# Gathered rows of a PEER feed-forward: a nearer place in the scheduler's order during the dense pass, and 5.15 instead of 5.25 rows per chunk

## The chip, the cores and the metric

One core of a Trainium2 chip runs the whole program. The metric is the device time of one execution in microseconds (us). The engines are TensorE (PE, whose weight loads are shown apart as PEld), VectorE (DVE), ScalarE (ACT), GpSimd (POOL) and SyncE (SP). SP issues the plain transfers and POOL the indirect ones; both kinds share the core's 16 DMA engines.

## What is computed

One decoder block on 1024 tokens of width 1024, in float32: two token mixers (stick-breaking attention and a gated delta rule) are merged by sigmoid gates, and a PEER feed-forward follows. For each token PEER picks 8 x 16 = 128 of 16384 experts, and adds their outputs, weighted by a gate and an exact GELU:

```
def block(args):
    hb, eb, gb = args                 # 128 tokens
    u = u_tab[eb]                     # 128 rows of 1024 for each token
    act = jax.nn.gelu(jnp.einsum('td,ted->te', hb, u), approximate=False)
    v = v_tab[eb]
    return jnp.einsum('te,ted->td', gb * act, v)
```

## The kernel before

The 1024 tokens are eight blocks of 128. PEER is done in two ways at once.

**Dense, blocks 2, 3, 6 and 7 (`dense`, L854).** All 16384 experts are evaluated for 512 tokens, and a table of gates that is zero for the experts not picked weighs them. There are 128 steps of 128 experts. A step has 24 matmuls of scores (L885, L887), a GELU on ACT (L889), a multiplication by the gates on DVE (`weigh`, L915) and a split of the product into two float32r halves, the high one on ACT (L919), the low one on DVE (L906), and 24 matmuls with V (`mm3`, L72 to L74). U and V arrive in 512 KB transfers, and each is split the same way (`split`, L63 on ACT, L64 on DVE). The loop over `k` (L966) has two `k` per step, and this pair is a **chunk**. After every eight `k`, four chunks, four accumulators of TensorE are added into `d_acc` by four DVE instructions (L974): the work between two such quads is a **group** below. TensorE can't write on before they are done, since six banks serve four accumulators.

**Gathered, blocks 0, 1, 4 and 5 (`gather_rows`, L993).** For each of the 128 picks of a block, POOL issues an indirect DMA that brings one row of U for each token (L1016, 128 rows of 4 KB, 512 KB), and DVE multiplies it with the hidden state and sums along it (L1019); this is a **u row**. After 128 of them a GELU follows (L1007) and a multiplication by the gates (L1009), and then 128 **v rows**, each an indirect DMA and a DVE instruction that adds into an accumulator (L1021). Below, a **row** is one such pair. There are 4 x 256 = 1024. The hidden state (from `h2d`) and the accumulator (from `x2d`) share one buffer, `gb_h`; when a block goes from u to v rows, or one block follows another, DVE waits for the load of the other. Rows land in buffers that are used in turn: four, `gb_row0` to `gb_row3`, and two more, `gb_row4` and `gb_row5`, while the dense loop runs (L961, L988). POOL issues in order, and a row's transfer starts once DVE has finished the row that had its buffer before.

**What sets the order.** The rows have no place of their own: `gather(phase)` (L1045) is called from every phase, adds `PACE[phase]` (L31) to a debt and emits one row for each whole unit of it. In the dense loop it is called once per chunk (L985), before that in the table of gates (L850), among others. A scheduler then orders each engine: of the instructions that are ready in its own reckoning it takes the one with the lowest number, and an instruction's number is the place at which it was emitted. `later(n)` (L46) adds n to the numbers of what is emitted inside it. Rows got 1000000, so that anything else that was ready went first. `behind` (L1032) keeps a row's DVE instruction behind the last DVE instruction that was emitted before it. The call without a phase, after the dense pass, emits the rows that are left, with no addition and, by then, four buffers.

Of the kernel before, what the change touches and what calls it, by code (L numbers as in the profile page):

```python
# [27 lines left out]
CB = 256  # L28
EPS = 1e-6

PACE = dict(sb=2.2, gdn=1.5, logits=2.5, merge=2.5, out=0.5, route=0, table=0.1, dense=5.25)  # L31
NEG = -1e30
C_Q, C_K, C_V = 0, 1024, 2048
C_GQ, C_GK, C_GV, C_GZ = 3072, 4096, 5120, 6144
# [4 lines left out]
class Block:  # L39
# [1005 lines left out]
    def gather(self, phase=None):  # L1045

        if self.rows is None:
            return
        if phase is None:
            self.anchor = None  # L1050
            for _ in self.rows:
                pass
            return
        self.due += PACE[phase]
        self.anchor = self.last_dve()
        with self.later(1000000):
            while self.due >= 1:
                self.due -= 1
                next(self.rows, None)
# [119 lines left out]
```

## Time and profile before

| | |
|---|---|
| median of 3 runs | 3876.8 us (3871.88 to 3877.51) |
| the profiled execution | 3877.26 us |
| its span, first to last instruction | 3875.4 us |
| dense pass, last quad of the gate tables to the end | about 2380 to 3875 us |
| first and last accumulation into `d_acc` (L974) | 2458 and 3853 us |

The profiled execution stands 0.5 us above the median. All moments below are us from the start of the span. A row of the timeline gives start, duration, engine, line, operation, output and inputs, the number of merged instructions, and in brackets the idle time of the engine before it with what ended it.

### The profile page before, as it was taken

What the parts mean: (1) busy time and instruction counts of PE and PEld (TensorE: products, weight loads), DVE (VectorE), ACT (ScalarE), POOL (GpSimd) and SP (SyncE); (2) the same over time, 40 slices, a digit from 0 to 9 for tenths busy, and PEclk for the clock granted to TensorE, in tenths of its full rate; (3) what the DMA queues carried; (4) which work ended last, traced back from release to release, by engine and by line L of the source; (5) the groups of instructions that cost most, each with busy time, mean ns of one, the idle gap of its engine ahead of it and who ended that gap; (6) DMA issues with size and microseconds to landing.
All of it is one profiled execution on the core that took longest, in us unless ns stands there. A gap on an engine that the chain in (4) does not pass through costs nothing.

```text
span 3875.4 us, 53560 instructions
## 1 busy us (share of the span) xinstructions
PE 3596.4 (93%) x18936; PEld 2983.8 (77%) x18936; DVE 3077.5 (79%) x6196; ACT 1740.7 (45%) x3846; POOL 1356.6 (35%) x1034
## 2 busy tenths in 40 slices
PE   8999999999999999998878877999999999999996
PEld 7878888788777688886667666787778787788785
DVE  5345554349988878888879998899898899899898
ACT  6755554333777655553322786222222322222221
POOL 0000000000044332223442003666666665676665
PEclk9999999999999999999989999999999999999998
DMA  4221113553377756558985568999999999999998
GB/s 121 88 82 50 55 50 115 174 186 93 96 256 265 246 191 192 191 182 290 325 307 170 158 185 289 353 361 358 334 365 358 345 371 365 348 364 374 353 359 312
DMA packets 344205, 937.49 MB, mean 242 GB/s; under 512 B 41984, under 2 KB 121088, under 8 KB 339712
## 3 DMA queue, kind: packets, MB, share of 16 engines
q0 software_dynamic: 147456, 536.94, 38.8%
q1 hardware_dynamic: 196480, 397.13, 30.1%
q8 instruction: 149, 2.44, 0.3%
q14 instruction: 120, 0.98, 0.1%
HBM read 864.22 MB, written 69.21 MB: 241 GB/s over the span
## 4 chain that ended last, share of the span: by engine, by line
PE 42%; issue 20%; POOL 12%; DVE 11%; DMA 10%; ACT 4%; SPq 0%; POOLq 0%; DVEq 0%; ACTq 0%
POOL gb_row L1016 12%; PE mm L72 6%; PE mm L74 6%; PE mm L73 6%; DMA gb_row<-peer_v,expert 5%; PE pc L848 3%; DMA gb_row<-peer_u,expert 3%; PE mm L885 2%; PE pz L532 2%; PE pz L526 2%; DVE gb_row L1019 2%; DVE w_lo L64 2%; PE mm L887 1%; PE pc L317 1%; PE pz L295 1%
## 5 line engine op out<-in xcount | busy, mean ns | idle before, releaser
L1016 POOL DMA_INDIRECT gb_row<-peer_u,expert x512 | 693.6, 1355 | 1848.2 <-DVE expert L793 1012.8
L1016 POOL DMA_INDIRECT gb_row<-peer_v,expert x512 | 661.9, 1293 | 656.4 <-DVE gb_h L1021 408.8
L1019 DVE SCALAR_TENSOR_TENSOR gb_row<-gb_row,gb_h 128x1024 f32<-128x1024 f32 x512 | 614.0, 1219 | 133.2 <-DMA gb_row<-peer_u,expert 109.7
L1021 DVE SCALAR_TENSOR_TENSOR gb_h<-gb_row,gb_act,gb_h 128x1024 f32<-128x1024 f32 x512 | 657.7, 1285 | 73.7 <-DMA gb_row<-peer_v,expert 50.4
L885 PE MATMUL mm<-hf,ut 128*128 128x512 f32 x2048 | 491.2, 391 | 6.9 <-DMA hf<-hd 6.9
L919 ACT CAST d_a<-u_act 128x512 fp32r<-128x512 f32 x128 | 79.2, 621 | 926.5 <-DVE u_act L915 917.7
L885 PEld LDWEIGHTS mm<-hf,ut 128*128 128x128 f32 x2048 | 386.1, 189 | 87.7 <-issue 7.6
L64 DVE TENSOR_TENSOR w_lo<-w_raw,w_hi 128x512 fp32r<-128x512 f32 (+1 forms) x450 | 297.6, 682 | 163.9 <-ACT w_hi L63 125.9
L63 ACT CAST w_hi<-w_raw 128x512 fp32r<-128x512 f32 (+1 forms) x450 | 262.1, 620 | 286.2 <-PE mm L73 122.6
L72 PE MATMUL mm<-h,w_hi 128*128 128x512 f32 (+1 forms) x784 | 322.9, 412 | 3.0 <-ACT pj L598 3.0
L74 PE MATMUL mm<-h,w_lo 128*128 128x512 f32 (+1 forms) x784 | 320.6, 409 | 0.0
L73 PE MATMUL mm<-h,w_hi 128*128 128x512 f32 (+1 forms) x784 | 319.7, 408 | 0.0
L72 PE MATMUL pz<-d_v,d_a 128*128 128x512 f32 x680 | 272.8, 401 | 41.2 <-DVE d_acc L974 30.1
L72 PE MATMUL mm<-w_hi,h 128*128 128x256 f32 x1024 | 299.8, 293 | 8.5 <-DVE x L647 5.7
L74 PE MATMUL mm<-w_hi,h 128*128 128x256 f32 x1024 | 294.0, 288 | 4.0 <-DVE h L64 4.0
L73 PE MATMUL mm<-w_lo,h 128*128 128x256 f32 x1024 | 295.1, 288 | 1.0 <-DVE w_lo L64 0.9
L74 PE MATMUL pz<-d_v,d_a 128*128 128x512 f32 x680 | 270.4, 398 | 0.0
L73 PE MATMUL pz<-d_v,d_a 128*128 128x512 f32 x680 | 270.4, 398 | 0.0
L887 PE MATMUL mm<-hf,ut 128*128 128x512 f32 x1024 | 257.0, 391 | 2.5 <-DVE ut L64 2.5
L887 PEld LDWEIGHTS mm<-hf,ut 128*128 128x128 f32 x1024 | 192.8, 188 | 42.8 <-DVE ut L64 3.3
L72 PEld LDWEIGHTS mm<-w_hi,h 128*128 128x128 f32 x1024 | 199.5, 195 | 16.3 <-DVE x L647 6.4
L73 PEld LDWEIGHTS mm<-w_lo,h 128*128 128x128 f32 x1024 | 199.7, 195 | 6.7 <-issue 3.8
(327 smaller groups left out, 7947.9 us busy)
## 6 DMA issues: line engine op xcount, KB each, us to landing
w_raw<-w_in SPq DMA_DIRECT2D x144, 512.0 KB
u_raw<-u_t SPq DMA_DIRECT2D x128, 512.0 KB
v_raw<-v_t SPq DMA_DIRECT2D x128, 512.0 KB
g_d<-gt_stg SPq DMA_DIRECT2D x16, 2048.0 KB
d_g<-g_d SPq DMA_DIRECT2D x31, 1024.0 KB
w_raw<-peer_w_q SPq DMA_DIRECT2D x32, 512.0 KB
gl<-pj SPq DMA_DIRECT2D x32, 256.0 KB
th<-gl SPq DMA_DIRECT2D x32, 256.0 KB
```

What stands on the lines that cost most here:

```text
L63: nc.scalar.copy(hi, src)
L64: nc.vector.tensor_tensor(lo, src, hi.bitcast(F32), op=OP.subtract)
L72: mm(out, l[0], r[0], start=first, stop=False)
L73: mm(out, l[0], r[1], start=False, stop=False)
L74: mm(out, l[1], r[0], start=False, stop=last)
L848: self.last_gate = mm(pg[:, u - u0], o2[:, u], o1[:, u], start=True, stop=True)
L885: mm(ps, ut[0][:, k], hx[a][:, k, x0:], start=k + a == 0, stop=False)
L887: mm(ps, ut[1][:, k], hx[0][:, k, x0:], start=False, stop=k == KD - 1)
L919: nc.scalar.copy(hi, act)
L1016: nc.gpsimd.indirect_dma_start(out=r, out_offset=None, in_=self.i["peer_u" if p < n else "peer_v"][0], in_offset=bass.IndirectOffsetOnAxis ...
L1019: i = nc.vector.scalar_tensor_tensor(r, r, 1.0, h2, op0=OP.mult, op1=OP.mult, accum_out=act[:, q:q + 1])
L1021: i = nc.vector.scalar_tensor_tensor(acc, r, act[:, q:q + 1], acc, op0=OP.mult, op1=OP.add)
```

## The change

In the dense pass alone the rows' numbers are raised by 800 instead of 1000000, and the debt grows by 5.15 per chunk instead of 5.25. Everything else of the program is as it was; the counts on every engine are the same.

```
-PACE = dict(sb=2.2, gdn=1.5, logits=2.5, merge=2.5, out=0.5, route=0, table=0.1, dense=5.25)
+PACE = dict(sb=2.2, gdn=1.5, logits=2.5, merge=2.5, out=0.5, route=0, table=0.1, dense=5.15)
...
         self.due += PACE[phase]
         self.anchor = self.last_dve()
-        with self.later(1000000):
+        with self.later(800 if phase == "dense" else 1000000):
             while self.due >= 1:
                 self.due -= 1
                 next(self.rows, None)
```

PE's and POOL's orders keep their forms, DVE's moves in many places. Three of them are shown, with buffer numbers.

**Start of the dense loop, DVE.** `gb_row1_22120` and `gb_row2_22380` were emitted in the gate tables, so they keep 1000000; the rows from `gb_row3_22834` on come from the dense loop. Before:

```order
L1019 SCALAR_TENSOR_TENSOR gb_row2_22380,gb_act_17073<-gb_row2_22380,gb_h2_17071 128x1024
L1019 SCALAR_TENSOR_TENSOR gb_row3_22834,gb_act_17073<-gb_row3_22834,gb_h2_17071 128x1024
L1019 SCALAR_TENSOR_TENSOR gb_row4_22837,gb_act_17073<-gb_row4_22837,gb_h2_17071 128x1024
L1019 SCALAR_TENSOR_TENSOR gb_row1_22828,gb_act_17073<-gb_row1_22828,gb_h2_17071 128x1024
L1019 SCALAR_TENSOR_TENSOR gb_row5_22840,gb_act_17073<-gb_row5_22840,gb_h2_17071 128x1024
L64 TENSOR_TENSOR d_v1_22846<-v_raw_22843,d_v0_22845 128x1024
L64 TENSOR_TENSOR ut1_22876<-u_raw_22873,ut0_22875 128x1024
L64 TENSOR_TENSOR d_v1_22929<-v_raw_22926,d_v0_22928 128x1024
L1019 SCALAR_TENSOR_TENSOR gb_row2_22831,gb_act_17073<-gb_row2_22831,gb_h2_17071 128x1024
L1019 SCALAR_TENSOR_TENSOR gb_row0_22911,gb_act_17073<-gb_row0_22911,gb_h2_17071 128x1024
L1019 SCALAR_TENSOR_TENSOR gb_row1_22914,gb_act_17073<-gb_row1_22914,gb_h2_17071 128x1024
```

Now:

```order
L1019 SCALAR_TENSOR_TENSOR gb_row1_22120,gb_act_17073<-gb_row1_22120,gb_h2_17071 128x1024
L64 TENSOR_TENSOR d_v1_22846<-v_raw_22843,d_v0_22845 128x1024
L64 TENSOR_TENSOR ut1_22876<-u_raw_22873,ut0_22875 128x1024
L64 TENSOR_TENSOR d_v1_22929<-v_raw_22926,d_v0_22928 128x1024
L1019 SCALAR_TENSOR_TENSOR gb_row4_22923,gb_act_17073<-gb_row4_22923,gb_h2_17071 128x1024
L1019 SCALAR_TENSOR_TENSOR gb_row1_22828,gb_act_17073<-gb_row1_22828,gb_h2_17071 128x1024
L1019 SCALAR_TENSOR_TENSOR gb_row2_22380,gb_act_17073<-gb_row2_22380,gb_h2_17071 128x1024
L64 TENSOR_TENSOR ut1_22959<-u_raw_22956,ut0_22958 128x1024
L915 TENSOR_TENSOR u_act_22904<-u_act_22904,d_g_22759 128x512
L906 TENSOR_TENSOR d_a1_22908<-u_act_22904,d_a0_22907 128x512
L1019 SCALAR_TENSOR_TENSOR gb_row1_22914,gb_act_17073<-gb_row1_22914,gb_h2_17071 128x1024
```

The two early rows, and with them whatever follows in buffers 1 and 2, stand behind later rows of the other buffers. `gb_row1_22828` needs buffer 1 from `gb_row1_22120`, and stands two rows behind it where it was four; `gb_row1_22914` stands two behind `gb_row1_22828`.

**Second change from u to v rows, DVE** (block 4; L1009 is the multiplication by the gates, and `gb_h2_27499` or `gb_h2_27571` the accumulator that has just been loaded). Before:

```order
L1019 SCALAR_TENSOR_TENSOR gb_row3_27493,gb_act_25419<-gb_row3_27493,gb_h2_25417 128x1024
L1009 TENSOR_TENSOR gb_act_25419<-gb_act_25419,gate4_428 128x128
L64 TENSOR_TENSOR d_v1_27513<-v_raw_27510,d_v0_27512 128x1024
L1021 SCALAR_TENSOR_TENSOR gb_h2_27499<-gb_row4_27501,gb_act_25419,gb_h2_27499 128x1024
L1021 SCALAR_TENSOR_TENSOR gb_h2_27499<-gb_row5_27504,gb_act_25419,gb_h2_27499 128x1024
L64 TENSOR_TENSOR ut1_27547<-u_raw_27544,ut0_27546 128x1024
L915 TENSOR_TENSOR u_act_27481<-u_act_27481,d_g_27139 128x512
L1021 SCALAR_TENSOR_TENSOR gb_h2_27499<-gb_row0_27507,gb_act_25419,gb_h2_27499 128x1024
L974 TENSOR_TENSOR d_acc_22731<-pc_27256,d_acc_22731 128x512
```

Now:

```order
L1019 SCALAR_TENSOR_TENSOR gb_row3_27565,gb_act_25419<-gb_row3_27565,gb_h2_25417 128x1024
L1009 TENSOR_TENSOR gb_act_25419<-gb_act_25419,gate4_428 128x128
L64 TENSOR_TENSOR ut1_27619<-u_raw_27616,ut0_27618 128x1024
L1021 SCALAR_TENSOR_TENSOR gb_h2_27571<-gb_row4_27573,gb_act_25419,gb_h2_27571 128x1024
L915 TENSOR_TENSOR u_act_27555<-u_act_27555,d_g_27124 128x512
L1021 SCALAR_TENSOR_TENSOR gb_h2_27571<-gb_row5_27576,gb_act_25419,gb_h2_27571 128x1024
L906 TENSOR_TENSOR d_a1_27559<-u_act_27555,d_a0_27558 128x512
L1021 SCALAR_TENSOR_TENSOR gb_h2_27571<-gb_row0_27579,gb_act_25419,gb_h2_27571 128x1024
L64 TENSOR_TENSOR d_v1_27672<-v_raw_27669,d_v0_27671 128x1024
```

Before, one split (L64) stands in front of the first v row and it is the last chunk of a group, with L974 a few rows on; now the first v row has a split in front of it too, the low half (L906) follows after two v rows, and it is the first chunk of a group.

**End of the program, POOL.** The last rows. Before:

```order
L1016 DMA gb_row4_33471<-peer_v,expert5_435 128x1024
L1016 DMA gb_row5_33474<-peer_v,expert5_435 128x1024
L1016 DMA gb_row0_33477<-peer_v,expert5_435 128x1024
L1016 DMA gb_row1_33480<-peer_v,expert5_435 128x1024
L1016 DMA gb_row2_33507<-peer_v,expert5_435 128x1024
L1016 DMA gb_row3_33510<-peer_v,expert5_435 128x1024
L1016 DMA gb_row4_33513<-peer_v,expert5_435 128x1024
L1016 DMA gb_row5_33516<-peer_v,expert5_435 128x1024
L1016 DMA gb_row0_33519<-peer_v,expert5_435 128x1024
L1016 DMA gb_row1_33550<-peer_v,expert5_435 128x1024
```

Now:

```order
L1016 DMA gb_row3_33520<-peer_v,expert5_435 128x1024
L1016 DMA gb_row4_33523<-peer_v,expert5_435 128x1024
L1016 DMA gb_row0_33543<-peer_v,expert5_435 128x1024
L1016 DMA gb_row1_33546<-peer_v,expert5_435 128x1024
L1016 DMA gb_row2_33537<-peer_v,expert5_435 128x1024
L1016 DMA gb_row3_33540<-peer_v,expert5_435 128x1024
L1016 DMA gb_row5_33526<-peer_v,expert5_435 128x1024
L1016 DMA gb_row2_33549<-peer_v,expert5_435 128x1024
L1016 DMA gb_row3_33552<-peer_v,expert5_435 128x1024
L1016 DMA gb_row0_33555<-peer_v,expert5_435 128x1024
```

Before, all rows were emitted inside the loop and go round six buffers to the end. Now ten rows (`gb_row2_33537` to `gb_row3_33564`) are emitted behind the loop, on four buffers and without an addition, and four of them stand in front of `gb_row5_33526`, which has 800. DVE's order there is `gb_row4_33523`, `gb_row5_33526`, `gb_row2_33537`. Counted on DVE, 370 rows stood before the first accumulation, 643 (269 u rows and 374 v rows) from there to the last, and 11 behind it; now it is 369, 632 (270 and 362) and 23.

## Rows read from the trace of the kernel before

**Rows 1.** The page: the span, busy time by engine, and four lines of the 40 slices (busy tenths of PE and DVE, granted TensorE clock, DMA share).

```profile
span 3875.4 us, 53560 instructions
...
PE 3596.4 (93%) x18936; PEld 2983.8 (77%) x18936; DVE 3077.5 (79%) x6196; ACT 1740.7 (45%) x3846; POOL 1356.6 (35%) x1034
...
PE   8999999999999999998878877999999999999996
DVE  5345554349988878888879998899898899899898
PEclk9999999999999999999989999999999999999998
DMA  4221113553377756558985568999999999999998
```

**Rows 2.** Busy time by stretch. Columns: stretch, its length, busy us (instructions) of PE, PEld, DVE, ACT, POOL, then granted clock, DMA share, GB/s. The first is first to last accumulation, the next two are groups with u rows, the fourth is one with v rows, the last is from the last accumulation to the end.

```profile
2458.40:3853.20 1394.80, 1341.06 (x5802) 1100.29 (x5802) 1275.29 (x1524) 376.81 (x484) 898.37 (x644) 0.98 0.95 355
3430.30:3474.10 43.80, 43.80 (x195) 36.27 (x194) 40.84 (x63) 12.91 (x16) 31.29 (x21) 1.00 0.99 379
3474.10:3517.10 43.00, 43.00 (x191) 35.60 (x190) 40.98 (x63) 12.92 (x16) 29.17 (x21) 1.00 0.98 377
3700.60:3745.60 45.00, 44.15 (x194) 35.96 (x192) 42.56 (x42) 12.15 (x17) 28.34 (x21) 1.00 0.95 358
3853.20:3875.40 22.20, 0.00 (x0) 0.00 (x0) 14.11 (x12) 0.00 (x0) 5.95 (x5) 0.50 0.75 293
```

**Rows 3.** Groups of instructions from the first to the last accumulation (2458.4 to 3853.2). Columns: line, engine, operation, count, busy us and mean ns of one, idle time before with its releasers.

```profile
L1016 POOL DMA_INDIRECT gb_row<-peer_v,expert x379 | 509.8, 1345 | 306.2 <-DVE gb_h L1021 223.5 <-issue 64.1 <-DMA gb_row<-peer_v,expert 9.7
L1016 POOL DMA_INDIRECT gb_row<-peer_u,expert x265 | 388.5, 1466 | 190.8 <-DVE gb_row L1019 123.8 <-issue 63.8 <-DVE gb_h L1021 3.2
L1021 DVE SCALAR_TENSOR_TENSOR gb_h<-gb_row,gb_act,gb_h 128x1024 f32<-128x1024 f32 x374 | 481.2, 1287 | 44.6 <-DMA gb_row<-peer_v,expert 22.3 <-DMA gb_h<-x2d 15.9
L1019 DVE SCALAR_TENSOR_TENSOR gb_row<-gb_row,gb_h 128x1024 f32<-128x1024 f32 x271 | 322.2, 1220 | 50.7 <-DMA gb_row<-peer_u,expert 28.5 <-DMA gb_h<-h2d 20.0 <-issue 1.2
```

**Rows 4.** Waits in the same stretch: engine, tile and line, what it waited for, us in total, times, longest.

```profile
POOL gb_row L1016 <- DVE gb_h L1021: 226.8, 165, 9.8
...
PE pz L72 <- DVE d_acc L974: 30.1, 14, 4.8
...
DVE gb_row L1019 <- DMA gb_row<-peer_u,expert: 28.5, 30, 2.3
...
DVE gb_h L1021 <- DMA gb_row<-peer_v,expert: 22.3, 19, 2.1
...
DVE d_a L906 <- ACT d_a L919: 22.0, 32, 0.7
...
DVE gb_row L1019 <- DMA gb_h<-h2d: 20.0, 2, 11.5
...
PE pc L72 <- DVE d_acc L974: 18.7, 7, 6.2
...
DVE gb_h L1021 <- DMA gb_h<-x2d: 15.9, 3, 7.7
...
PE pz L72 <- ACT d_a L919: 3.5, 2, 2.9
```

**Rows 5.** Timeline of DVE at the start of the dense loop: rows 353 (`gb_row1_22120`), 357 (`gb_row1_22828`), 359 and 362 of the 1024.

```profile
2421.35 1.22 DVE L1019 SCALAR_TENSOR_TENSOR gb_row<-gb_row,gb_h 128x1024 f32<-128x1024 f32 x1
...
2430.55 1.22 DVE L1019 SCALAR_TENSOR_TENSOR gb_row<-gb_row,gb_h 128x1024 f32<-128x1024 f32 x1 [3.93 <-DMA gb_row<-peer_u,expert]
...
2436.25 1.21 DVE L1019 SCALAR_TENSOR_TENSOR gb_row<-gb_row,gb_h 128x1024 f32<-128x1024 f32 x1
...
2444.59 1.23 DVE L1019 SCALAR_TENSOR_TENSOR gb_row<-gb_row,gb_h 128x1024 f32<-128x1024 f32 x1 [3.08 <-DMA gb_row<-peer_u,expert]
```

**Rows 6.** Timeline of DVE at the first and the second change from u to v rows in the dense pass: the split between, and the first v row with its wait for the accumulator.

```profile
2487.18 1.22 DVE L64 TENSOR_TENSOR ut<-u_raw,ut 128x1024 fp32r<-128x1024 f32 x1
...
2493.85 1.29 DVE L1021 SCALAR_TENSOR_TENSOR gb_h<-gb_row,gb_act,gb_h 128x1024 f32<-128x1024 f32 x1 [5.45 <-DMA gb_h<-x2d]
...
3059.41 2.60 DVE L1021 SCALAR_TENSOR_TENSOR gb_h<-gb_row,gb_act,gb_h 128x1024 f32<-128x1024 f32 x2 [7.72 <-DMA gb_h<-x2d]
```

**Rows 7.** Timeline of DVE from the last accumulation on: the last eleven rows.

```profile
3853.20 6.66 DVE L1021 SCALAR_TENSOR_TENSOR gb_h<-gb_row,gb_act,gb_h 128x1024 f32<-128x1024 f32 x5
...
3861.58 1.28 DVE L1021 SCALAR_TENSOR_TENSOR gb_h<-gb_row,gb_act,gb_h 128x1024 f32<-128x1024 f32 x1 [1.72 <-DMA gb_row<-peer_v,expert]
...
3864.10 1.28 DVE L1021 SCALAR_TENSOR_TENSOR gb_h<-gb_row,gb_act,gb_h 128x1024 f32<-128x1024 f32 x1 [1.24 <-DMA gb_row<-peer_v,expert]
...
3866.61 5.24 DVE L1021 SCALAR_TENSOR_TENSOR gb_h<-gb_row,gb_act,gb_h 128x1024 f32<-128x1024 f32 x4 [1.23 <-DMA gb_row<-peer_v,expert]
```

**Rows 8.** Timeline of POOL in the mixers of the second half, where four buffers serve: the first and the thirteenth of thirteen issues in the densest such stretch.

```profile
1563.74 1.86 POOL L1016 DMA_INDIRECT gb_row<-peer_v,expert  x1 [6.32 <-DVE g_t L577]
...
1585.82 0.94 POOL L1016 DMA_INDIRECT gb_row<-peer_v,expert  x1 [0.73 <-DVE g_nrm L476]
```

More of the change, by code (lines that the diff above doesn't have):

```diff
@@ L29 @@
 EPS = 1e-6
-PACE = dict(sb=2.2, gdn=1.5, logits=2.5, merge=2.5, out=0.5, route=0, table=0.1, dense=5.25)
+PACE = dict(sb=2.2, gdn=1.5, logits=2.5, merge=2.5, out=0.5, route=0, table=0.1, dense=5.15)
 NEG = -1e30
@@ L1055, in gather @@
         self.anchor = self.last_dve()
-        with self.later(1000000):
+        with self.later(800 if phase == "dense" else 1000000):
             while self.due >= 1:
```

## Prediction, made before the changed kernel ran

> **What bounds the kernel now.** I read the page first, then busy time by stretch, the groups and the waits of the dense loop, and last the timeline of three places. On the page [rows 1] TensorE is busy 93% of the span, so it looks like the bound; but in the dense pass DVE stands at 8 to 9 tenths too and the DMA engines at 9. The stretches show how close the three lie [rows 2]. A group with u rows takes 43.0 to 43.8 us, and TensorE is busy in all of it: 43.0 us is its pace. A group with v rows takes 45.0 us, TensorE is idle 0.85 us of it, DVE is busy 42.56 us, and the transfers move 358 GB/s. From the first accumulation to the last, 1394.8 us, TensorE is idle 53.7 us, and the waits name 30.1 + 18.7 us of it as waits for the accumulation on DVE and 3.5 us for the split product [rows 4]. DVE itself waits for rows (28.5 + 22.3 us), for the loads of `gb_h` (20.0 + 15.9 us) and for ACT (22.0 us) [rows 4], and for nothing of TensorE's that is listed. So DVE's queue, its work and these waits, sets the loop's time, with TensorE a per cent or two behind it: what shortens DVE's queue helps until a group comes down to 43 us. Behind the last accumulation TensorE has nothing left; the end is eleven v rows [rows 7].
>
> The sum below is made against the profiled execution, 3877.3 us, which is 0.5 us above the median of the runs shown. A difference under 0.2%, 7.8 us, counts as none.
>
> **Rows taken out of the loop.** Between first and last accumulation DVE has 12 v rows fewer and one u row more. A v row takes 1.287 us and a u row 1.220 us [rows 3]: -15.4 + 1.2 = -14 us. That is all gain if DVE stays the last to be ready. Bounds: nothing, if every group were at TensorE's pace already, as the two u groups shown are; and, if the six buffers were the limit, the v group's own pace, 45.0 us for 21 rows or 2.14 us each: 11 x 2.14 = -24 us. I take -14: the v group shown, busy 42.56 of 45.0 us, is nearest to a full DVE. No transfer is added or lost. The 800 itself I price at nothing in the loop: in the middle of a block the rows still stand behind all dense work that is ready, and the chunk's pattern is the old one, so it needs no cover.
>
> **The second change from u to v rows.** There DVE waited 7.72 us for the accumulator, against 5.45 us at the first change, where a split of 1.22 us ran in between [rows 6]. Now the second looks like the first: -2 us. Ends: 0, since the load may simply come that much later, and -7.7, the whole wait.
>
> **Start of the loop.** The order of the rows costs something here. A row can't start its transfer before the row that had its buffer is done. Before, row 357 stood four rows behind that one and row 362 three; from release to use they took 8.0 us (row 353 starts at 2421.35 and takes 1.22; row 357 starts at 2430.55) and 7.1 us (row 359 ends at 2437.46; row 362 starts at 2444.59), and DVE was idle 3.93 and 3.08 us [rows 5]. From row 366 on the distance was six. Now rows 360, 362 and 370 stand two behind, row 364 three, and rows 356, 357, 366 and 368 four. I laid DVE's new order out by hand, with 1.14 us from one u row or split to the next, 0.6 us for the shorter ones, and 7.1 us from a release to the use: waits of 3.1, 2.6, 3.7 and 2.4 us before the first accumulation. That is 11.8 against 7.0 us, with one u row less (-1.2): +3.6 us; row 370 adds 1.8 behind it. With 8.0 us it comes to about +10. I take +6. The low end is 0, if TensorE's lead of some chunks takes it all. The DVE instructions queued behind a waiting row are the splits of U and V and the accumulation, and TensorE waits for the last.
>
> On the same step the Trainium skill (DMA: Bandwidth & Descriptors, "Anatomy of one DMA") gives for such a transfer a fixed 2.0 us and its bytes over 436 GB/s, which for 512 KB is an estimate of 3.2 us. By that no row at distance two would wait, the start would cost 0, and the sum would be 7 us instead of 13. The 7.1 and 8.0 us of this trace disagree: beside other transfers a row takes twice as long.
>
> **The end.** Behind the last accumulation there were 11 rows: the first five had landed, the others came with gaps of 1.2 to 1.7 us, and the last ended at 3871.85, 18.65 us on [rows 7]. Now there are 23. The two that follow on six buffers I price like the eleven, 18.65 / 11 = 1.7 us each: 3.4. Then ten rows go round four buffers. The densest stretch with four shows twelve issues in 22.1 us, 1.84 us each [rows 8]: 18.4 if they ran from the start like that. One more thing happens: `gb_row5_33526` is issued behind four rows that DVE needs later, the last of which needs the buffer of the row two before it. With four buffers a release and the use lie 4 x 1.84 - 1.29 = 6.1 us apart, and DVE has one row to do meanwhile: it waits about 5 us, while the four land; they go through at 1.29 us each, which gives back 4 x 0.55 = 2.2 us. Its price is thus +3, and the sum 24.8. From this I take off 2 us: the four 512 KB stores of `d_acc` lie in the first half of the end in both programs, so its second half has less beside it. +23 us. The ends: 12 x 1.287 = 15 us, if no row waits any more, and 12 x 2.5 = 30 us, the spacing of the single rows at 3861.58, 3864.10 and 3866.61. TensorE and ACT are idle there, so nothing covers it.
>
> **Sum:** +6 - 14 - 2 + 23 = +13 us, 3877.3 + 13 = **3890 us**: the end grows by more than the loop gives back, since at the end only one of the three resources is in use.
>
> **The rivals.**
>
> *The loop comes down to TensorE's pace (faster).* Rows wait 50.8 us in the loop [rows 4] with nearly full buffers. If 0.4 rows less per group lets half of these waits go, the loop gains 25 us more: 3890 - 25 = 3865. For it: the three resources lie within 2 us of each other, and TensorE has 53.7 us of idle time to give back, with the clock lowered after the long ones. Against it: the u groups at full pace have such waits too, and waits for rows follow the bursts (three rows on end between two splits), which stay as they were. It decides from 21 us of waits saved on, 13 for the sum and 8 for the bound of a difference. Chance 0.18.
>
> *The transfers set the pace throughout (no difference).* The bytes are the same, and at 0.95 to 0.99 the DMA engines are as full as TensorE. Then a row costs what it transfers: 0.524 MB at 377 GB/s is 1.39 us. Loop -11 x 1.39 = -15, end +12 x 1.39 = +17, start and change nothing: +2, 3879 us. Against it: in the v group the engines are at 0.95, and the last stretch has 293 GB/s [rows 2], so the end isn't filled by transfers. A rule that speaks for it stands in the Trainium skill (DMA: Bandwidth & Descriptors, "Specifications"): a core gets some 358 GB/s of memory bandwidth. That is the v group's figure to the digit, but the u groups' 377 and 379 GB/s lie above it, so it isn't a wall here. With the lower price at the start (sum 7, 3884 us) these cases share a chance of 0.27.
>
> *The start tears a larger hole (slower than forecast).* If each of the four near rows exposes its full 8.0 us less one u row, 6.8 us, that is 27 us in place of the 7 us of before: +20 instead of +6, 3904 us, and more where TensorE's waits lower its clock. Chance 0.05; what I forecast has 0.50.
>
> **How the numbers follow.** The likeliest case is the forecast, 3890 us, with ends of its own from about 3880 (loop -24) to 3900 (end +30, start +10). To leave out no more than 2 in 10, the range reaches down to the faster case, 3865, and up to 3905, just over the large hole. Faster by over 0.2% (below 3869): the first rival and a little of the unknown of the loop's price, 0.20. Within 0.2%: 0.27 and the forecast's low part, less what it loses to the sides, 0.27. Slower: 0.53.
>
> **What would show it.** Right, step by step: the last accumulation comes at about 3843 (3853 + 6 - 14 - 2), and from there to the last v row it takes some 42 us, not 18.65, with one wait of DVE near 5 us before the row in `gb_row5`. The first accumulation comes about 4 us later than 2458, with three or four waits for u rows above 2 us before it. v groups take about 44.5 us. Wrong: if the waits of DVE for rows in the loop fall from 50.8 us to 30 or less, the loop is worth more than I said, and if the end takes under 35 us, the rows there cost less than four buffers let me believe.

## The result, and the profile after

| | before | after |
|---|---|---|
| median, same chip | 3874.7 us (3871.9 to 3877.5, 4 runs) | 3903.4 us (3901.2 to 3906.0, 4 runs) |
| ratio, 95% interval | | 1.0074 (1.0057 to 1.0092) |
| the profiled execution, and its span | 3877.3, 3875.4 us | 3902.9, 3901.1 us |

The changed kernel is 0.7% slower, 22 to 36 us. The forecast was +13 us in a range up to +28 against its profiled execution; the two profiled executions differ by 25.7 us of span. Cut into stages, the span shows where they arise. From the first score matmul (L885) to the first accumulation it takes 333.6 us instead of 329.1 (**+4.5**), from first to last accumulation 1390.2 instead of 1394.8 (**-4.5**), from there to the end of the last row 44.8 instead of 18.65 (**+26.2**); the rest differs by -0.5. The page answers to [rows 1]:

```profile
span 3901.1 us, 53536 instructions
...
PE 3601.5 (92%) x18936; PEld 2985.4 (77%) x18936; DVE 3080.2 (79%) x6196; ACT 1737.0 (45%) x3846; POOL 1350.1 (35%) x1034
...
PE   8999999999999999998878878999999999999994
...
DVE  5345554449988878888789997899889999889897
...
DMA  4221113552387756568985669999999999999998
```

Little in it tells of the change: DVE is busy as long as before, and only TensorE's last slice falls, from 6 tenths to 4. The stretches tell more. They answer to [rows 2]; the first is the loop, then one group with v rows, one with u rows, and the end.

```profile
2462.40:3852.70 1390.30, 1340.35 (x5802) 1098.61 (x5802) 1263.45 (x1512) 373.33 (x483) 886.03 (x633) 0.98 0.94 351
3700.40:3745.20 44.80, 44.56 (x196) 36.35 (x195) 42.56 (x42) 12.13 (x18) 28.17 (x21) 1.00 0.94 355
3474.00:3518.00 44.00, 43.94 (x194) 36.33 (x195) 41.45 (x64) 12.06 (x16) 31.29 (x22) 1.00 0.98 371
3852.70:3901.10 48.40, 0.00 (x0) 0.00 (x0) 29.55 (x24) 0.00 (x0) 19.32 (x17) 0.52 0.72 261
```

In the loop DVE is busy 11.8 us less (1275.3 to 1263.5), near the 14 reckoned for 11 rows fewer, but it is idle 7.3 us more (119.5 to 126.8), so the loop is only 4.5 us shorter. The waits of the loop, which answer to [rows 4], show where the rest went:

```profile
PE pz L72 <- DVE d_acc L974: 36.6, 15, 6.9
DVE d_a L906 <- ACT d_a L919: 32.3, 47, 0.7
DVE gb_row L1019 <- DMA gb_row<-peer_u,expert: 31.8, 28, 3.5
DVE gb_h L1021 <- DMA gb_row<-peer_v,expert: 20.9, 14, 2.5
DVE gb_row L1019 <- DMA gb_h<-h2d: 18.9, 2, 9.7
...
PE pc L72 <- DVE d_acc L974: 13.4, 7, 6.7
DVE gb_h L1021 <- DMA gb_h<-x2d: 9.9, 3, 3.5
```

The low half waits 0.69 us for ACT in 47 chunks instead of 32, 10.3 us more; rows wait 52.7 us instead of 50.8, the loads of `gb_h` 28.8 instead of 35.9.

Three places answer to [rows 5], [rows 6] and [rows 7]. DVE at the start of the loop, the rows that waited:

```profile
2429.56 1.23 DVE L1019 SCALAR_TENSOR_TENSOR gb_row<-gb_row,gb_h 128x1024 f32<-128x1024 f32 x1 [3.69 <-DMA gb_row<-peer_u,expert]
...
2438.02 1.22 DVE L1019 SCALAR_TENSOR_TENSOR gb_row<-gb_row,gb_h 128x1024 f32<-128x1024 f32 x1 [1.53 <-DMA gb_row<-peer_u,expert]
...
2446.56 1.23 DVE L1019 SCALAR_TENSOR_TENSOR gb_row<-gb_row,gb_h 128x1024 f32<-128x1024 f32 x1 [3.05 <-DMA gb_row<-peer_u,expert]
...
2450.58 1.23 DVE L1019 SCALAR_TENSOR_TENSOR gb_row<-gb_row,gb_h 128x1024 f32<-128x1024 f32 x1 [1.64 <-DMA gb_row<-peer_u,expert]
...
2460.71 1.23 DVE L1019 SCALAR_TENSOR_TENSOR gb_row<-gb_row,gb_h 128x1024 f32<-128x1024 f32 x1 [2.51 <-DMA gb_row<-peer_u,expert]
```

The first v row behind the second change from u to v, and the end:

```profile
3068.54 1.29 DVE L1021 SCALAR_TENSOR_TENSOR gb_h<-gb_row,gb_act,gb_h 128x1024 f32<-128x1024 f32 x1 [3.54 <-DMA gb_h<-x2d]
...
3852.71 6.55 DVE L1021 SCALAR_TENSOR_TENSOR gb_h<-gb_row,gb_act,gb_h 128x1024 f32<-128x1024 f32 x5
3860.50 1.28 DVE L1021 SCALAR_TENSOR_TENSOR gb_h<-gb_row,gb_act,gb_h 128x1024 f32<-128x1024 f32 x1 [1.24 <-DMA gb_row<-peer_v,expert]
3863.84 7.89 DVE L1021 SCALAR_TENSOR_TENSOR gb_h<-gb_row,gb_act,gb_h 128x1024 f32<-128x1024 f32 x6 [2.06 <-DMA gb_row<-peer_v,expert]
3879.03 6.57 DVE L1021 SCALAR_TENSOR_TENSOR gb_h<-gb_row,gb_act,gb_h 128x1024 f32<-128x1024 f32 x5 [7.30 <-DMA gb_row<-peer_v,expert]
3887.06 1.28 DVE L1021 SCALAR_TENSOR_TENSOR gb_h<-gb_row,gb_act,gb_h 128x1024 f32<-128x1024 f32 x1 [1.46 <-DMA gb_row<-peer_v,expert]
```

The wait of 7.30 us stands before the row in `gb_row5`. POOL in that stretch shows why: the issue for that row, at 3872.84, is the last of five, and the next one waits until DVE has used the row behind it.

```profile
3866.72 1.86 POOL L1016 DMA_INDIRECT gb_row<-peer_v,expert  x1 [3.72 <-DVE gb_h L1021]
...
3872.84 0.94 POOL L1016 DMA_INDIRECT gb_row<-peer_v,expert  x1 [0.30 <-issue]
3881.90 1.86 POOL L1016 DMA_INDIRECT gb_row<-peer_v,expert  x1 [8.12 <-DVE gb_h L1021]
```

From the first of the five issues until the row is used, the DMA engines are busy 0.82 of the time (columns as in [rows 2]); in the stretch just before, with the stores of `d_acc` beside the rows, they are full and move 420 GB/s:

```profile
3866.72:3879.03 12.31, 0.00 (x0) 0.00 (x0) 4.91 (x5) 0.00 (x0) 5.84 (x5) 0.50 0.82 286
...
3862.00:3866.70 4.70, 0.00 (x0) 0.00 (x0) 2.79 (x3) 0.00 (x0) 0.93 (x1) 0.50 1.03 420
```

### The profile page after: what moved, and what is told of

Its sections match the earlier page's. It is cut to its first block, busy times and chain, and to the rows that moved or that the text cites. A ratio compares the mean times of both kernels' runs of the same rounds, so it can differ in the third digit from the quotient of the medians.

```text
span 3901.1 us, 53536 instructions
## 1 busy us (share of the span) xinstructions
PE 3601.5 (92%) x18936; PEld 2985.4 (77%) x18936; DVE 3080.2 (79%) x6196; ACT 1737.0 (45%) x3846; POOL 1350.1 (35%) x1034
## 4 chain that ended last, share of the span: by engine, by line
PE 36%; issue 24%; POOL 14%; DMA 11%; DVE 11%; ACT 4%; SPq 0%; POOLq 0%; DVEq 0%; ACTq 0%
POOL gb_row L1016 14%; PE mm L72 6%; PE mm L73 6%; PE mm L74 6%; DMA gb_row<-peer_v,expert 5%; PE pc L848 3%; DMA gb_row<-peer_u,expert 2%; PE pz L532 2%; PE pz L526 2%; DVE w_lo L64 2%; DVE gb_row L1019 1%; DVE gb_h L1021 1%; PE pz L295 1%; PE pc L317 1%; PE pz L522 1%
## 5 line engine op out<-in xcount | busy, mean ns | idle before, releaser
L885 PE MATMUL mm<-hf,ut 128*128 128x512 f32 x2048 | 490.5, 391 | 6.9 <-DMA hf<-hd 6.9
L885 PEld LDWEIGHTS mm<-hf,ut 128*128 128x128 f32 x2048 | 385.7, 188 | 87.4 <-issue 7.6
L64 DVE TENSOR_TENSOR w_lo<-w_raw,w_hi 128x512 fp32r<-128x512 f32 (+1 forms) x450 | 297.7, 682 | 164.1 <-ACT w_hi L63 125.7
L72 PEld LDWEIGHTS mm<-w_hi,h 128*128 128x128 f32 x1024 | 200.5, 196 | 15.3 <-DVE x L647 5.5
L74 PEld LDWEIGHTS mm<-w_hi,h 128*128 128x128 f32 x1024 | 200.4, 196 | 7.7 <-DVE h L64 5.8
```

The source lines that it names most:

```text
L64: nc.vector.tensor_tensor(lo, src, hi.bitcast(F32), op=OP.subtract)
L72: mm(out, l[0], r[0], start=first, stop=False)
L74: mm(out, l[1], r[0], start=False, stop=last)
L885: mm(ps, ut[0][:, k], hx[a][:, k, x0:], start=k + a == 0, stop=False)
```

## The experiments

All are edits of the kernel before or of the changed one. The table has the stages of every trace, in us: up to the first score matmul, from there to the first accumulation, the loop with its rows (counted on DVE) between first and last accumulation, and from there to the end of the last row with the rows there. Ratios are to the kernel before, with 95% intervals.

| | up to L885 | start | loop (rows) | end (rows) | span | ratio |
|---|---|---|---|---|---|---|
| before | 2129.3 | 329.1 | 1394.8 (643) | 18.65 (11) | 3875.4 | |
| e5, before again | 2128.0 | 328.3 | 1395.0 (643) | 18.8 (11) | 3873.6 | 0.9996 (0.9986-1.0007) |
| changed | 2128.9 | 333.6 | 1390.2 (632) | 44.8 (23) | 3901.1 | 1.0074 (1.0057-1.0092) |
| e1, 5.15 alone | 2127.9 | 328.0 | 1391.6 (631) | 45.8 (23) | 3896.8 | 1.0058 (1.0039-1.0077) |
| e2, 800 alone | 2128.8 | 331.7 | 1403.3 (644) | 18.5 (11) | 3885.8 | 1.0034 (1.0023-1.0045) |
| e3, six buffers | 2137.5 | 330.8 | 1391.5 (632) | 34.8 (23) | 3898.2 | 1.0063 (1.0045-1.0082) |
| e4, low half later | 2125.4 | 320.3 | 1392.5 (642) | 24.5 (16) | 3866.2 | 0.9976 (0.9963-0.9989) |
| e6, 5.0 | 2125.7 | 328.1 | 1358.5 (613) | 77.8 (41) | 3893.7 | 1.0058 (1.0042-1.0073) |
| e7, e4 with 5.0 | 2133.8 | 319.6 | 1368.0 (612) | 88.0 (46) | 3912.9 | 1.0074 (1.0059-1.0090) |
| e8, 5.35 | 2131.9 | 327.4 | 1408.5 (654) | none | 3873.6 | 0.9979 (0.9970-0.9988) |
| e9, U split, changed | 2133.1 | 333.4 | 1399.3 (632) | 45.1 (23) | 3914.5 | 1.0067 (1.0044-1.0090) |
| e10, U split, before | 2127.5 | 330.1 | 1395.0 (643) | 18.2 (11) | 3874.3 | 1.0015 (1.0003-1.0028) |
| e11, e10 with 5.35 | 2132.0 | 329.1 | 1415.6 (654) | none | 3883.0 | 1.0009 (0.9994-1.0023) |
| e12, half rows | 2112.4 | 315.5 | 1346.8 (630) | 33.0 (23) | 3811.2 | 0.9814 (0.9776-0.9851) |

**e5: how steady the stages are.** The kernel before, unchanged.

> The kernel before once more, unchanged, for a second trace: it tells how far the length of a stage differs between two executions of one program. Theory (the stages are fixed by the order, only the first phases drift): first to last accumulation 1394.8 +-2 us, from the last accumulation to the last row 18.65 +-1 us, ratio of times 1.000. Rival (the loop itself drifts): the loop is more than 5 us off, and then the loop's -4.5 us in the changed kernel and its +8.5 us with the priority alone mean nothing.

Measured: loop and end differ by 0.2 us each. On the way the two traces agree less well: counted from the first score matmul, the twelfth quad of accumulations (L974) comes 3.1 us earlier in the second trace and the 24th 4.1 us later. A second pair of this kind is the changed kernel and e3 below, which has the same DVE order up to the last accumulation: its start is 330.8 us instead of 333.6, its loop 1391.5 instead of 1390.2, so that the changed loop is 3.3 to 4.8 us shorter than that of before over the four traces. So I take differences between loops or starts as shown from about 5 us on, and smaller ones where several traces agree. What varies most is the time before the dense pass, up to 12 us between programs whose edits do not touch it (2125.4 to 2137.5). That is why a stage tells more here than the whole time.

**e1 and e2: each half of the change alone.**

```
e1: -dense=5.25
    +dense=5.15
e2: -        with self.later(1000000):
    +        with self.later(800 if phase == "dense" else 1000000):
```

> The kernel before with 5.15 rows per chunk alone; rows keep 1000000. Theory (pace and priority cost in different places): no scramble at the start, so the first accumulation stays at 2458 us; loop about 4 us shorter than before, with some 47 waits of the low half (L906) for ACT as in the changed kernel; 23 rows at the end in about 45 us with one wait over 5 us. Time: before + 22 us. Rival (the priority of 800 spoils the loop): the loop gives back the 14 us of the 12 rows, time before + 12 us.

> The kernel before with the addition of 800 alone; 5.25 rows per chunk. Theory: the start as in the changed kernel, first accumulation at about 2462 us, loop and end as before (11 rows, 18.7 us): before + 4 us. Rival (the priority spoils the loop): the loop is 10 us or more longer than before: before + 14 us.

Measured: 5.15 alone makes +22 us (15 to 30), as the theory had it, and by its terms: the loop gains 3.2 us where it said 4 and the rival 14, and the end costs 27. The 800 alone makes +13 (9 to 17), more than the theory's 4 and about the rival's 14: the start costs 2.6 us, and the loop 8.5. The second quad of accumulations comes 383.6 us after the first score matmul, where it is 377.8 and 377.1 in the two traces of before and 377.1 in e1; the changed kernel and e3 have 382.3. So the order at the start costs 4 to 6 us in all, part of it behind the first accumulation. The other 5 us that e2's loop loses are open.

**e3: the end on six buffers.** The changed kernel, with the rows that are left emitted, with 800, before two buffers are given up:

```
+            with self.later(800):
+                self.gather()
             del self.row_bufs[4:]
```

> The changed kernel, with the ten left-over rows emitted inside the dense pass, on six buffers and with the addition of 800, so that the end is in order. Theory (four buffers and the order make the end dear): start and loop as in the changed kernel, the 23 rows of the end in 18.7 + 12 x 1.6 = 38 us instead of 44.8, no wait above 3 us: before + 19 us, 7 less than the changed kernel. Rival (a row of the end costs what POOL and the transfers take, whatever the buffers): the end stays at 45 us, before + 26 us.

Measured, DVE at the end:

```profile
3859.85 5.24 DVE L1023 SCALAR_TENSOR_TENSOR gb_h<-gb_row,gb_act,gb_h 128x1024 f32<-128x1024 f32 x4
3865.38 1.28 DVE L1023 SCALAR_TENSOR_TENSOR gb_h<-gb_row,gb_act,gb_h 128x1024 f32<-128x1024 f32 x1 [0.29 <-DMA gb_row<-peer_v,expert]
3867.90 1.29 DVE L1023 SCALAR_TENSOR_TENSOR gb_h<-gb_row,gb_act,gb_h 128x1024 f32<-128x1024 f32 x1 [1.24 <-DMA gb_row<-peer_v,expert]
3870.99 1.28 DVE L1023 SCALAR_TENSOR_TENSOR gb_h<-gb_row,gb_act,gb_h 128x1024 f32<-128x1024 f32 x1 [1.80 <-DMA gb_row<-peer_v,expert]
3872.88 11.99 DVE L1023 SCALAR_TENSOR_TENSOR gb_h<-gb_row,gb_act,gb_h 128x1024 f32<-128x1024 f32 x9 [0.60 <-DMA gb_row<-peer_v,expert]
3885.40 9.21 DVE L1023 SCALAR_TENSOR_TENSOR gb_h<-gb_row,gb_act,gb_h 128x1024 f32<-128x1024 f32 x7 [0.53 <-DMA gb_row<-peer_v,expert]
```

The wait of 7.3 us is gone, and 23 rows take 34.8 us, 1.5 us each. So of the 26 us at the end, 10 are four buffers with the row out of turn, and 16 are twelve more rows. The whole time doesn't show the 10 us: this execution was 8.6 us late before the dense pass began, and the intervals of the two ratios overlap.

**e6 and e8: more steps of the same number.** 5.0 and 5.35 in the kernel before. With 5.35 no row is left at the end.

> The kernel before with 5.0 rows per chunk: 30 rows fewer in the loop (613), 41 at the end, and in DVE's order the low half stands directly behind its multiplication in 64 chunks of 32 before. Theory (each such pair makes DVE wait 0.69 us for ACT): the loop gets 30 x 1.287 = 38.6 us shorter by the rows and 32 x 0.69 = 22 us longer by the waits, 1394.8 -> 1378; the waits of the low half for ACT rise from 22 to 44 us. Rival (full price of a row, the waits are free): 1356. Rival (TensorE or something else than these waits keeps the loop long): 1385 or more. The end in all: from 18.65 to about 79 us (23 rows took 45.8, 18 more at 1.84), so about +44 us in time by the theory, ratio 1.011.

> The kernel before with 5.35 rows per chunk: the last eleven rows go into the loop (654), the accumulation stands behind the last row, and the low half directly behind its multiplication in 20 chunks instead of 32. Theory: loop +11 x 1.287 - 12 x 0.69 = +6 us, end -18.65 us and in its place the stores of the accumulator alone, some 5 to 8 us behind it instead of 3.5: in all -8 to -11 us, ratio 0.997 to 0.998. Rival (full price of a row in the loop, +14): +0 us, ratio 1.000. Rival (TensorE gets starved by the longer DVE queue, clock down): slower.

Measured in e6, the loop and its waits:

```profile
2453.80:3812.30 1358.50, 1330.99 (x5802) 1097.57 (x5802) 1241.70 (x1494) 381.71 (x484) 872.44 (x615) 0.99 0.94 353
...
DVE d_a L906 <- ACT d_a L919: 44.5, 65, 0.7
DVE gb_row L1019 <- DMA gb_row<-peer_u,expert: 23.3, 23, 3.2
...
DVE gb_h L1021 <- DMA gb_row<-peer_v,expert: 7.7, 8, 1.8
```

The theory is wrong. The waits for ACT rose as it said, to 44.5 us, and the loop became 36.3 us shorter all the same, the rival's 1356 within 3 us, since the waits for rows fell from 50.8 to 31.0. For TensorE, 26 of these 36 us are idle time (53.7 to 27.5) and 10 are busy time (1341.1 to 1331.0 for the same matmuls, with the granted clock at 0.99 instead of 0.98). In e8 the loop grew by 13.7 us, also the full price. From 654 to 613 rows the loop changes by 50.0 us, 1.22 us a row, and 5.25 lies on the straight line between (1395.1 by it); but 5.15 lies 8.5 to 11 us above it, in the changed kernel, e1 and e3 alike. DVE's idle time in the loop says the same: 119.5 us before, 116.8 in e6, 120.0 in e8, but 126.8 to 129.5 in the three with 5.15. The line is that of one layout and three points: in e10 and e11 below eleven rows make 20.6 us, 1.87 a row, in e4 and e7 thirty rows 24.5 us, 0.82 a row. Rearranging alone moves the loop by about as much as 5.15 is off.

**e4 and e7: the low half without a wait for ACT.**

```
-                    nc.vector.tensor_tensor(lo, act, ...)
+                    w = self.last_dve()
+                    i = nc.vector.tensor_tensor(lo, act, ...)
+                    self.behind(i, w)
```

> The kernel before, with the low half of a split product (L906) kept behind the next chunk's weighing, so that it never waits for ACT. Theory (DVE's queue sets the loop's time, waits for ACT included): the 22 us of waits of L906 for ACT in the loop go to about 0 and the loop gets 15 to 22 us shorter; 16 rows are left at the end instead of 11, + 8 us: before - 7 to - 14 us. Rival (TensorE's pace or the transfers set the loop): waits for rows grow by as much, the loop stays within 5 us, time before + 3 to + 8 us.

> The last experiment's low half kept behind the DVE instruction emitted before it (L906 no longer waits for ACT), and 5.0 rows per chunk: 612 rows in the loop where that kernel had 642, 46 at the end. Theory (the waits for ACT are what ate the price of the rows): without them the loop falls by the full 30 x 1.287 = 38.6 us, 1392.5 -> 1354. Rival (something else eats it): it falls by 10 to 20 us, to 1372 to 1383. End from 24.5 to about 87 us in both, so +24 us against the kernel with 5.25 by the theory, about 3894 us on this scale, +45 by the rival.

Measured: e4 is faster, 0.9976, as the theory forecast, but its loop is only 2.3 us shorter, as the rival had it, though without the rival's longer waits for rows (50.1 us). The gain of 8.8 us stands before the first accumulation. In the loop the 22 us of waits for ACT are gone, and TensorE waits 46 us for the low half, which now comes late. e7 decides nothing: its loop falls by 24.5 us, between both answers, and there the splits of U wait 44.8 us for ACT, a wait that neither theory had.

**e9 to e11: the wait for ACT, taken away.** A chunk's split of U is put between L915 and L906. The rows themselves stay in order, but they bunch, since the split no longer stands between them: in the loop 35 bursts of four rows stand on end instead of 20 in e9, and 26 instead of 10 in e10.

```
                 self.split(ut[0], ut[1], raw)
+                if len(weighed) >= 1:
+                    self.behind(self.last_split, weighed[-1])
```

(`last_split` is the split's DVE instruction, `weighed` the list of the L915.)

> The changed kernel with one edit: the split of U of a chunk (L64, 1.14 us) is kept behind the last multiplication (L915), so that in DVE's order it stands between L915 and the low half (L906) in nearly every chunk; L906 stands directly behind L915 in 5 chunks instead of 52. Rows, their numbers and the 23 rows at the end are as in the changed kernel. Theory (the waits of L906 for ACT, 32 us with 5.15 rows and 22 with 5.25, are time of DVE's queue and took back what the rows gave): they fall to 3 us or less, DVE's other waits stay, and the loop of 1390.3 us gets 10 to 29 us shorter, at least to the 1381 us that 632 rows would make at 1.22 us each. Time 10 to 25 us under the changed kernel's. Rival (rows wait for their transfers instead, the sum of waits stays): waits for rows rise from 53 us to 70 or more, the loop stays within 4 us of 1390.

> The same edit in the kernel before (5.25 rows, 1000000): L906 directly behind L915 in 4 chunks instead of 35, 11 rows at the end. Theory: the 22 us of waits for ACT go, the loop of 1394.8 us gets 8 to 20 us shorter, and so does the time: ratio 0.995 to 0.998. Rival (waits for transfers take their place): loop within 4 us of 1395, ratio 1.000, waits for rows up from 51 us to 68 or so.

> That edit with 5.35 rows per chunk, so that no row is left at the end. Theory: the gain of the edit (8 to 20 us) and that of 5.35 rows (8 us measured) add up less 8 us of waits for ACT that 5.35 rows had taken away already: 3856 to 3868 us where the kernel before has 3879, ratio 0.994 to 0.997, the fastest so far. Rival: as 5.35 rows alone, 0.998.

Measured in e9 (the lines are moved on by 3 or 4):

```profile
DVE gb_row L1023 <- DMA gb_row<-peer_u,expert: 62.2, 50, 4.8
...
DVE gb_h L1025 <- DMA gb_row<-peer_v,expert: 26.1, 24, 1.8
...
DVE d_a L909 <- ACT d_a L923: 1.4, 2, 0.7
```

And in e10:

```profile
DVE gb_row L1023 <- DMA gb_row<-peer_u,expert: 46.2, 47, 4.5
...
DVE gb_h L1025 <- DMA gb_row<-peer_v,expert: 18.1, 21, 1.6
...
DVE d_a L909 <- ACT d_a L923: 0.7, 1, 0.7
```

The rival's mechanism holds, twice. The waits for ACT fell from 32.3 to 1.4 us and from 22.0 to 0.7, and rows wait 88.3 us instead of 52.7 and 64.3 instead of 50.8. The loop is 9 us longer in the one, where the rival allowed 4, and the same in the other, 1395.0. What DVE doesn't wait for ACT, it waits for a transfer. How much of that is the bunching of the rows these runs can't tell. e11 gains nothing either.

**e12: rows of half the bytes.**

```
-  indirect_dma_start(out=r, ..., in_=self.i[...][0],
+  indirect_dma_start(out=r[:, D // 2:], ..., in_=self.i[...][0].rearrange("e (h d) -> (e h) d", h=2),
+  r2 = r[:, None, D // 2:].to_broadcast([P, 2, D // 2])     (read in place of r)
```

> The changed kernel with rows of half the bytes: each gather brings 512 columns, 2 KB for a token, from a view of the table with half as long rows, and DVE reads these 512 columns twice, so that its instructions keep 1024 elements; what is summed is another thing than the reference. 630 rows in the loop, 23 at the end, the low half directly behind its multiplication in 57 chunks of 52. Only the loop and the end are read. Theory (DVE's waits in the loop stand for the transfers, so that a wait taken away in one place comes back in another): waits for rows fall from 53 us to 15 or less although those of the low half stay at 32 to 39, and the loop of 1390.3 us comes down to 1345 to 1365, TensorE's own 1340 being its floor; the end goes from 44.8 us to 33 to 38. Rival (the order and the hand-over set them, the time from a release to the issue and landing hardly depends on bytes): waits for rows stay above 35 us, the loop above 1378, the end above 41.

Measured, the loop and its waits, and DVE at the end:

```profile
2427.90:3774.70 1346.80, 1329.83 (x5823) 1097.72 (x5821) 1259.82 (x1510) 387.61 (x485) 915.14 (x631) 0.99 0.74 240
...
DVE d_a L906 <- ACT d_a L919: 33.7, 49, 0.7
DVE gb_row L1021 <- DMA gb_row<-peer_u,expert: 20.3, 19, 4.3
...
DVE gb_h L1023 <- DMA gb_row<-peer_v,expert: 0.3, 1, 0.3
...
3774.66 17.13 DVE L1023 SCALAR_TENSOR_TENSOR gb_h<-gb_row,gb_act,gb_h 128x1024 f32<-128x1024 f32 x13
3792.81 5.29 DVE L1023 SCALAR_TENSOR_TENSOR gb_h<-gb_row,gb_act,gb_h 128x1024 f32<-128x1024 f32 x4 [1.02 <-DMA gb_row<-peer_v,expert]
```

In the loop the DVE order is that of the changed kernel but for some ten of 1241 instructions. The loop is 43 us shorter with the same DVE work. TensorE is idle 17 us of it instead of 50, and busy 1329.8 us instead of 1340.4, with the granted clock at 0.99 instead of 0.98; so 1340 was no floor. Waits for rows fell to 20.6 us, not quite to the 15 expected (v rows wait no more, u rows still 20), while those for ACT stayed at 33.7. At the end the wait of 7.3 us is 1.0, and 23 rows take 33.0 us. The loads of `gb_h`, whose size is unchanged, are waited for 17.2 us instead of 28.8. So bytes, not the hand-over, make most of the waits. Whether it is the sum of the bytes that binds, or the time of one transfer with six buffers to cover it, no run tells: none had more buffers.

## Why the prediction was right, and where it was not

**The end** (forecast +23, measured +26.2): right. The wait before the row in `gb_row5` was there, 7.3 us instead of about 5; e3 prices buffers and turn at 10 us together, and with half the bytes (e12) the wait is 1.0 us, so it is the transfers of five rows on end.

**The start** (forecast +6, with +3.6 before the first accumulation): right. That came 4.5 us later, and 1.7 in e3 with the same order; over the second quad it is 4.4 or 4.5 us in both against one trace of before and 5.1 or 5.2 against the other. e1, without the 800, has none of it. The waits were 3.7, 1.5, 3.1, 1.6 and 2.5 us where the hand layout had 3.1, 2.6, 3.7 and 2.4.

**The second change from u to v** (forecast -2): the wait fell by 4.2 us, from 7.72 to 3.54, the same sign and within the ends given, but the reason was wrong. A split ran in front of the first v row in the kernel before too (first line), and in e3, with the changed kernel's order, the wait was 5.90 us (second line). So some 2 us are common to both traces, and the rest differs between two executions.

```profile
3050.46 1.23 DVE L64 TENSOR_TENSOR d_v<-v_raw,d_v 128x1024 fp32r<-128x1024 f32 x1 [0.65 <-ACT d_v L63]
...
3078.82 1.28 DVE L1023 SCALAR_TENSOR_TENSOR gb_h<-gb_row,gb_act,gb_h 128x1024 f32<-128x1024 f32 x1 [5.90 <-DMA gb_h<-x2d]
```

**The rows taken out of the loop** (forecast -14): this step failed. With the second change the loop should have lost 16 us, and lost 4.5; the last accumulation, forecast for 3843, ended at 3852.7. The sentence that failed is "That is all gain if DVE stays the last to be ready". DVE's busy time did fall by 11.8 us, but its idle time grew by 7.3. DVE is not alone the last to be ready: it waits for rows, and e12 shows that the transfers make most of these waits; e9 and e10 fit that. Nor was the chunk's pattern the old one, as the pricing had it: the low half waits for ACT in 47 chunks instead of 32, in e1 in 49, so it comes from the pace and not from the 800. The average price, 1.22 us a row, is right from 5.35 over 5.25 to 5.0 (e6, e8); at 5.15 the loop lies 8.5 to 11 us above that line. I took the waits of the low half for ACT, up by 10.3 us, to be the cause; e6 speaks against it, where they rose by 22.5 us and the loop fell by the full price, and e9, where they went and the loop did not shorten. In the order of 5.15, 20 bursts of four rows stand on end, 10 with 5.25; but 5.0 has 21 of them and lies on the line, so that is not shown to be it. Why 5.15 falls above the line is open.

**The 800 "priced at nothing in the loop"**: e2 measured +8.5 us with 5.25, of which some 3 belong to the start; with 5.15 the loop is the same with the 800 (1390.2, and 1391.5 in e3) as without (1391.6 in e1). It depends on the arrangement. The times add up within their intervals: the changed kernel +28.7 us, e1 and e2 +22 and +13.

**The rivals.** That half of the row waits go did not happen at 5.15 (52.7 us), but nearly did at 5.0 (31.0), where the loop is 36 us shorter; that took a whole row per group (30 rows over 31 groups), not 0.4. The transfers were dismissed as a wall because groups of u rows run at 377 and 379 GB/s. The loops of this study with whole rows average 350 to 356 GB/s, whatever the rows, and half the bytes made the loop 43 us shorter: not a wall for a group, but a bound of the loop that weighs more than the forecast gave it. The rule of the Trainium skill that was weighed there (DMA: Bandwidth & Descriptors, "Specifications", some 358 GB/s for a core) is near these averages, and single groups exceed it, as does the 420 GB/s of the end.

The profiled execution came out 13 us above the forecast, 3902.9 for 3890 us: the loop and the second change together gave back 11.5 us less and the end cost 3 us more, the start 1.5 us less. That the time still lies in the range is luck in part: its upper end, 3905, was set for a larger hole at the start, which did not come.

## What to carry to other kernels

When two engines and the transfers are within a few per cent of each other, a wait that is taken off one queue can come back as a wait for another resource, as in e9 and e10: halve that resource's load in an experiment before you price what an instruction costs. A step of a pacing number changes the order everywhere. Neither one instruction's duration (1381 us for this loop) nor the line through the steps on either side (1382) gave the 1390 us of 5.15, so allow some 10 us for the arrangement or run the step itself. Work that was pushed out of this overlapped loop cost more at the end than it gave in the loop (e1, e6 and e7 too), so pace it to have nothing left: 5.35 rows per chunk was faster than both kernels (0.9979), and so was the low half moved later (0.9976).

## What the runs showed of the hardware that was not expected

- Two executions of one program agreed to 0.2 us in a stage of 1395 us, though in its middle they lay up to 4 us apart, and two of another order to 1.3 us. The time before the dense pass differed by 12 us between programs whose edits do not touch that part.
- In the loop of the changed kernel the low half waited 0.69 us for ACT's copy each of 47 times, and taking that wait away did not shorten the loop (e9).
- A row's gather at the end, alone but for four others issued just before it, took 6.2 us from its issue at 3872.84 until DVE could use it at 3879.03. The Trainium skill's formula (DMA: Bandwidth & Descriptors, "Anatomy of one DMA") gives an estimate of 3.2 us for one transfer of that size by itself; no run here had one by itself.
